# Three-product matmuls as two with [high|low] operands, and down projections in two halves of their outputs

## The chip, the cores and the metric

The kernel runs on one core of one Trainium2 chip. The metric is the device time of one execution in microseconds, the median of the runs shown. The core's engines are TensorE (PE in the profile; its weight loads have a row of their own, PEld), VectorE (DVE), ScalarE (ACT), GpSimd (POOL) and SyncE (SP), whose queue issues the weight transfers.

## The reference, cut to what matters

One sequence of 256 tokens with 1024 features passes through two layers of a first block and two layers of a second block, all in float32:

```python
# first block, per layer
x = x + concat(diff_attention, moba_attention) @ w_out
x = x + conv_ffn(rms_norm(x), w_up, conv_w, conv_b, w_down)   # silu(conv g) * (conv up), then down
# second block, per layer
x = x + 0.5 * swiglu(rms_norm_2(x), w_gate, w_up, w_down)
h = rms_norm_2(x); proj = h @ w_in + b_in
y_attn = forgetting_attention(q, k, v, log_f) @ w_o_attn
y_rnn = (rg_lru(conv(xr)) * gelu(gr)) @ w_o_rnn
x = x + (sigmoid(g_attn) * y_attn + sigmoid(g_rnn) * y_rnn) @ w_out
x = x + 0.5 * swiglu(rms_norm_2(x), ...)
```

All feed-forward layers are 2816 wide (22 tiles of 128), so there are six of them: two with the convolution and four gated ones (swiglu).

## The kernel before, in words

Activations lie with features on the partitions, in tiles of 128 features by 256 tokens. Every float32 operand of a large product is split into two float32r parts, high (a rounded copy) and low (the rest), and a product of two such operands is three matmuls that add into the same PSUM columns: high with high, high with low, low with high. `mm3` (line 419) issues them; each has its own weight load.

Weights come as a stream of chunks of 128 x 2048 float32 (1 MB), in the order in which they are used. `issue_dma` (line 234) transfers a chunk into one of NRAW = 4 raw buffers on SP's queue; `piece_h` and `piece_l` (lines 254, 268) split it in four pieces of 512 columns, the high part on ACT (tile `wh`), the low part on DVE (tile `wl`), into rings of three chunks. A raw buffer is free when its last piece is split.

- `proj` (line 529) multiplies one chunk, 8 contraction tiles by 2 output tiles, into one PSUM bank (tile `mm`): 16 calls of `mm3`. It serves the up projections (a chunk holds a gate tile and an up tile) and, in the second block's mixer, the projections x, a, n, r from the normalised operands `hH`, `hL` and the two output projections A (from `oH`) and R (from `rH`).
- `vpair` and `vproj` (lines 564, 545) multiply with the weights as the moving operand of 512, 256 or 264 columns (tile `mv`).
- `down` (line 585) adds two contraction tiles to all eight output tiles, which fill four banks (tile `acc`): again 16 calls of `mm3`. A feed-forward layer (`ffn`, line 633) alternates: two chunks up, one chunk down, the down being `lag` pairs behind (2 with the convolution, else 1). In the last chunk the order is by pairs of output tiles, and after each pair `boundary` (line 612) adds the sum to x (DVE, tile `x`), and `norm_pair` (line 480) makes the next stage's operands x*g in two parts (`xh` on ACT, `xl` on DVE) and the squares (`sq`, on ACT; their sum `ss` on POOL). The norm's factor `rstd` is applied later, when a projection's bank is read.

There are eight PSUM banks in all. During a feed-forward layer four are the accumulators and the others turn over among the up projections. After an up projection `evac_swiglu` (line 672) reads the bank once (DVE, `u<-mm,rstd`, which frees it), takes silu on ACT, multiplies on DVE and splits the result into `aH`, `aL` (`finish_act`, line 664). `make_evac_conv` (line 686) has a convolution of five more operations in between.

The order of all engines' work is written out by the program, from estimated times (class Estimate, line 69): PE's matmuls come in a fixed order, and between two tiles `substep` (line 346) puts splits and background units into the queues of ACT and DVE when the estimate says their operands are there. Each engine then runs its queue in order.

Of the kernel before, what the change touches and what calls it, by code (L numbers as in the profile page):

```python
# [25 lines left out]
NBLK = 40  # L26

# column layout of the packed per-partition vectors
# [38 lines left out]
class Estimate:  # L67
    """rough time at which each engine ends its emitted work and each tile is written:
    background work is put into the instruction streams about when its operands are there"""
# [7 lines left out]
    def key(self, x):  # L77
        """a tile, or a quarter of a chunk of weights"""
        w = self.wide.get(x.name)
        return x.name if w is None else (x.name, 4 * x.offset // w)  # L80

    def cost(self, eng, op, out, ins, kw):
# [3 lines left out]
        if eng == "pe":  # L86
            if op == "transpose":
                return 115.0
            f = 1.66 if ins[0].dtype == F32 else 0.418
            return max(107.0, f * w) + 2.0  # L90
# [53 lines left out]
def kernel(ctx: ExitStack, tc: tile.TileContext, t: dict):  # L144
# [29 lines left out]
    # ------------------------------------------------------------------ stream  # L174
    # every matrix is cut into chunks of 2048 columns per partition; a chunk is
    # loaded, split into two float32r parts, and used by the tensor engine.
    stream = []

    def phase_chunks():
        for l in range(L):  # L180
# [7 lines left out]
            ffn_chunks(t["w_up"], t["w_down"], l, 2)  # L188
        for l in range(L):
            ffn_chunks(t["w_gu1"], t["w_d1"], l, 1)  # L190
            wi = t["w_in2"]
            base = {"q": 0, "k": 4, "v": 8, "x": 12, "r": 16, "a": 20, "n": 24}
            for step in MIX2.split():
                if step == "q0":
                    stream.append(t["w_qf"][l])
                elif step == "G":
                    stream.append(t["w_g"][l])
                elif step in PAIRS:
                    stream.extend(t["w_p2"][l, PAIRS.index(step), i] for i in range(2))
                elif step[0] in "ARO":  # L200
                    stream.append(t[{"A": "w_oa", "R": "w_or", "O": "w_out2"}[step[0]]][l, int(step[1])])
                else:
                    stream.append(wi[l, base[step[0]] + int(step[1])])
            ffn_chunks(t["w_gu2"], t["w_d2"], l, 1)

    def ffn_chunks(u, d, l, lag):
        for j in range(NF // 2):
            stream.append(u[l, 2 * j])
            stream.append(u[l, 2 * j + 1])
            if j >= lag:  # L210
                stream.append(d[l, j - lag])
        for j in range(NF // 2 - lag, NF // 2):
            stream.append(d[l, j])
# [10 lines left out]
    NRAW = 4  # L224
# [6 lines left out]
    def wide(c):  # L231
        return stream[c].shape[-1]

    def issue_dma(parts=1, also=None):
# [7 lines left out]
        for i in range(parts):  # L242
            if also:
                also(i)
            nc.sync.dma_start(r[:, i * w:(i + 1) * w], stream[c][:, i * w:(i + 1) * w])
# [32 lines left out]
    def fill():  # L278
        """splits of coming chunks, as far as the vector and scalar engines have time for them"""
# [11 lines left out]
    def urgent():  # L291
        """one piece of the chunk that comes next"""
# [19 lines left out]
    # ------------------------------------------------------------- background  # L312
# [63 lines left out]
    # ----------------------------------------------------------------- consts  # L376
# [4 lines left out]
    X = [cpool.tile([P, 2, S], F32, name=f"x{i}") for i in range(4)]  # L381
    nv = VEC["early"]
# [8 lines left out]
    for p in range(4):  # L391
        est.R[X[p].name] = T0 - 500.0 + 2200.0 * p
# [16 lines left out]

    def small(w, name="sm"):  # L410
# [13 lines left out]
    # ------------------------------------------------------------------ norms  # L424
# [3 lines left out]
    def rsqrt(r, b, w):  # L428
        """r = 1 / sqrt(b + eps), with one Newton step"""
# [14 lines left out]
    def norm_tail(N):  # L444
        while N.ss is None or N.ss[1] < 4:
            yield POLL
        ssum = N.ss[0]
        (dve if N is norms[0] else pool).tensor_add(ssum[:, :S], ssum[:, :S], ssum[:, S:])
# [4 lines left out]
        pe.matmul(b[:, :S], ones_d, ssum[:, :S], start=True, stop=True)  # L453
# [4 lines left out]
        if N.tok:  # L458
            # the same by token: [token, half] and its square
# [11 lines left out]
            # eps / rstd^2: a norm of the unnormalised queries takes it in place of eps  # L471
# [8 lines left out]
    def norm_pair(N, p):  # L480
        """float32r parts of x*g of one pair of tiles, and the sum of squares"""
        yield W("act", X[p])
        xh = blk("xh", F32R)
        for m in range(2):
            act.activation(as2(xh)[:, m], X[p][:, m], AF.Identity, scale=v1(N.g, 2 * p + m))
        sq = squares(p)
        yield W("dve", xh)
        xl = blk("xl", F32R)
        for m in range(2):
            dve.scalar_tensor_tensor(as2(xl)[:, m], X[p][:, m], v1(N.g, 2 * p + m),  # L490
                                     as2(xh)[:, m].bitcast(F32), op0=ALU.mult, op1=ALU.subtract)
        N.H[p], N.L[p] = xh, xl
        add_squares(N, sq)

    def squares(p):
        sq = blk("sq")
        act.activation(sq, X[p].rearrange("p a b -> p (a b)"), AF.Square)
        return sq

    def add_squares(N, sq):  # L500
        if N.ss is None:
            N.ss = (sq, 1)
        else:
            s2 = blk("ss")
            pool.tensor_add(s2, N.ss[0], sq)
            N.ss = (s2, N.ss[1] + 1)

    def new_norm(g, tok=False):
        N = Norm()
        N.tok, N.rt, N.e2 = tok, None, None  # L510
        N.g, N.H, N.L, N.ss, N.rstd = g, [None] * 4, [None] * 4, None, None
        return N

    def k_tiles(H, Lo):
        def high(k):
            wait_for(lambda: Lo[k // 2] is not None)
            return as2(H[k // 2])[:, k % 2]
        return high, (lambda k: as2(Lo[k // 2])[:, k % 2])

    def x_update(p, acc, scale):  # L520
        xf = X[p].rearrange("p a b -> p (a b)")
        if scale == 1.0:
            dve.tensor_add(xf, acc, xf)
        else:
            dve.scalar_tensor_tensor(xf, acc, scale, xf, op0=ALU.mult, op1=ALU.add)
        unbank()

    # ------------------------------------------------------- projection kinds
    def proj(rh, rl):
        h, lo = next_chunk(None)  # L530
        h3 = h.rearrange("p (k c) -> p k c", k=KT)
        l3 = lo.rearrange("p (k c) -> p k c", k=KT)
# [3 lines left out]
        for k in range(KT):  # L536
            for m in range(2):
                ms = slice(m * P, (m + 1) * P)
                mm3(o[:, m], h3[:, k, ms], l3[:, k, ms], rh(k), rl(k),
# [5 lines left out]
    def vproj(hh, hl):  # L545
        """by token: one bank [token, half, 256], or one bank for each half of a wider chunk"""
        h, lo = next_chunk(None)
        h3 = h.rearrange("p (k c) -> p k c", k=KT)
        l3 = lo.rearrange("p (k c) -> p k c", k=KT)
# [5 lines left out]
        for k in range(KT):  # L555
            for m in range(2):
                ms = slice(m * P, (m + 1) * P)
                mm3(o[m], hh(k)[:, ms], hl(k)[:, ms], h3[:, k], l3[:, k],
# [5 lines left out]
    def vpair(hh, hl):  # L564
        """by token, 512 columns in two chunks: a bank for each half of the tokens"""
        wait_for(lambda: bank_any(2))
        bs = [bank("mv") for _ in range(2)]
        for half in range(2):
            h, lo = next_chunk(None)
            h3 = h.rearrange("p (k c) -> p k c", k=KT // 2)  # L570
            l3 = lo.rearrange("p (k c) -> p k c", k=KT // 2)
            for kk in range(KT // 2):
                k = half * (KT // 2) + kk
                for tt in range(2):
                    xh, xl = hh(k)[:, tt * P:(tt + 1) * P], hl(k)[:, tt * P:(tt + 1) * P]
# [9 lines left out]
    def down(acc, sh, sl, first, last, after=None):  # L585
        """adds two contraction tiles to all eight output tiles (four banks)"""
        h, lo = next_chunk(None)
        h3 = h.rearrange("p (k c) -> p k c", k=2)
        l3 = lo.rearrange("p (k c) -> p k c", k=2)

        def one(k, m):
            ms = slice(m * P, (m + 1) * P)
            mm3(as2(acc[m // 2])[:, m % 2], h3[:, k, ms], l3[:, k, ms], sh(k), sl(k),
# [8 lines left out]
        else:  # L602
            for p in range(4):
# [5 lines left out]
                after(p)  # L609
                substep()  # L610

    def boundary(acc, scale, N):
        """hooks for the last contraction: x update, and the next norm's operands"""
        def pair(p):
            yield W("dve", acc[p])
            if N is None:
                for m in range(2):
                    dve.scalar_tensor_tensor(X[p][:, m], as2(acc[p])[:, m], scale, X[p][:, m],
                                             op0=ALU.mult, op1=ALU.add)
                    nc.sync.dma_start(t["out"][p, :, m], X[p][:, m])  # L620
                unbank()
            else:
                x_update(p, acc[p], scale)
                yield from norm_pair(N, p)
                if p == 3:
                    spawn(norm_tail(N), front=True)

        def after(p):
            spawn(pair(p), front=True)
        return after  # L630

    # --------------------------------------------------------------------- ffn
    def ffn(N, evac, scale, N2, lag):
        rh, rl = k_tiles(N.H, N.L)
        acts = {}
        acc = []
# [985 lines left out]
```

## Time and profile before

| | us |
|---|---|
| median of 3 runs | 1920.77 |
| lowest, highest | 1915.81, 1922.2 |
| span of the profiled execution (first to last instruction; the page gives no other time of it) | 1916.7 |

In the profile, busy times of PE are of pipelined matmuls whose recorded durations overlap, so what a matmul costs is read from start to start. A timeline row gives start and duration in us, engine, line, operation, and output and inputs by the program's names; "[1.83 <-DVE xl L111]" is idle time before it and what ended it. Nearly all instructions have line 111, a recording helper, so they are told apart by their tiles.

### The profile page before, as it was taken

What the parts mean: (1) busy time and instruction counts of PE and PEld (TensorE: products, weight loads), DVE (VectorE), ACT (ScalarE), POOL (GpSimd) and SP (SyncE); (2) the same over time, 40 slices, a digit from 0 to 9 for tenths busy, and PEclk for the clock granted to TensorE, in tenths of its full rate; (3) what the DMA queues carried; (4) which work ended last, traced back from release to release, by engine and by line L of the source; (5) the groups of instructions that cost most, each with busy time, mean ns of one, the idle gap of its engine ahead of it and who ended that gap; (6) DMA issues with size and microseconds to landing.
All of it is one profiled execution on the core that took longest, in us unless ns stands there. A gap on an engine that the chain in (4) does not pass through costs nothing. (4 is left out here: it accounts for less than half of the span.)

```text
span 1916.7 us, 36939 instructions
## 1 busy us (share of the span) xinstructions
PE 1894.5 (99%) x14806; PEld 1837.7 (96%) x14806; DVE 1401.1 (73%) x2885; ACT 1170.5 (61%) x2811; POOL 58.8 (3%) x64
## 2 busy tenths in 40 slices
PE   9999999999999999999999999999999999999999
PEld 7899999899999999988999999999999899999999
DVE  7888778879878755589867755566657886866554
ACT  8866556867555644467786644454445677855443
POOL 2010001001000100010000100010001000000000
PEclk9999999999999999999999999999999999999999
DMA  9444555344555555554455455545555445545551
GB/s 290 170 154 167 186 190 184 132 155 137 196 196 176 177 176 181 193 199 165 155 186 191 173 180 184 188 156 196 177 181 208 174 154 174 181 175 198 183 191 67
DMA packets 49581, 340.05 MB, mean 177 GB/s; under 512 B 5836, under 2 KB 6900, under 8 KB 9216
## 3 DMA queue, kind: packets, MB, share of 16 engines
q1 hardware_dynamic: 47808, 330.19, 49.8%
q0 software_dynamic: 1456, 7.47, 1.4%
q8 instruction: 116, 1.90, 0.4%
q14 instruction: 57, 0.47, 0.1%
q10 hardware_dynamic: 144, 0.02, 0.0%
HBM read 336.30 MB, written 1.36 MB: 176 GB/s over the span
## 5 line engine op out<-in xcount | busy, mean ns | idle before, releaser
L111 ACT ACTIVATE wh<-raw 128x512 fp32r<-128x512 f32 x1248 | 709.4, 627 | 546.3 <-PE mm L111 203.9
L111 DVE TENSOR_TENSOR wl<-raw,wh 128x512 fp32r<-128x512 f32 x1248 | 807.3, 691 | 195.5 <-ACT wh L111 194.4
L111 PE MATMUL mm<-xl,wh 128*128 128x256 f32 x2112 | 600.4, 284 | 10.8 <-DVE xl L111 10.8
L111 PE MATMUL mm<-xh,wh 128*128 128x256 f32 x2112 | 601.5, 285 | 0.0
L111 PE MATMUL mm<-xh,wl 128*128 128x256 f32 x2112 | 599.9, 284 | 0.0
L111 PEld LDWEIGHTS mm<-xl,wh 128*128 128x128 f32 x2112 | 407.6, 193 | 12.4 <-DVE xl L111 12.0
L111 PEld LDWEIGHTS mm<-xh,wh 128*128 128x128 f32 x2112 | 407.7, 193 | 0.4
L111 PEld LDWEIGHTS mm<-xh,wl 128*128 128x128 f32 x2112 | 407.6, 193 | 0.0
L111 PE MATMUL acc<-aH,wh 128*128 128x256 f32 x1056 | 298.8, 283 | 0.0
L111 PE MATMUL acc<-aL,wh 128*128 128x256 f32 x1056 | 298.8, 283 | 0.0
L111 PE MATMUL acc<-aH,wl 128*128 128x256 f32 x1056 | 298.8, 283 | 0.0
L111 DVE TENSOR_TENSOR u<-mm,rstd 128x512 f32<-128x512 f32 x132 | 90.8, 691 | 223.6 <-PE mm L111 223.6
L111 PEld LDWEIGHTS acc<-aH,wh 128*128 128x128 f32 x1056 | 202.8, 192 | 0.0
L111 PEld LDWEIGHTS acc<-aL,wh 128*128 128x128 f32 x1056 | 202.8, 192 | 0.0
L111 PEld LDWEIGHTS acc<-aH,wl 128*128 128x128 f32 x1056 | 202.8, 192 | 0.0
L111 PE MATMUL mv<-wh,xl 128*128 128x512 f32 (+2 forms) x416 | 157.8, 379 | 3.3 <-DVE xl L111 3.3
L111 PE MATMUL mv<-wh,xh 128*128 128x512 f32 (+2 forms) x416 | 160.4, 386 | 0.2 <-ACT wh L111 0.2
L111 PE MATMUL mv<-wl,xh 128*128 128x512 f32 (+2 forms) x416 | 155.9, 375 | 0.0
L111 PE MATMUL mm<-hH,wh 128*128 128x256 f32 x512 | 145.9, 285 | 0.0
L111 PE MATMUL mm<-hH,wl 128*128 128x256 f32 x512 | 144.9, 283 | 0.0
L111 PE MATMUL mm<-hL,wh 128*128 128x256 f32 x512 | 144.8, 283 | 0.0
L111 PEld LDWEIGHTS mm<-hL,wh 128*128 128x128 f32 x512 | 98.2, 192 | 0.1
(218 smaller groups left out, 2789.5 us busy)
## 6 DMA issues: line engine op xcount, KB each, us to landing
raw<-in_w_gu SPq DMA_DIRECT2D x88, 1024.0 KB, 4.9
raw<-in_w_up SPq DMA_DIRECT2D x44, 1024.0 KB, 4.8
raw<-in_w_d SPq DMA_DIRECT2D x44, 1024.0 KB, 4.8
raw<-in_w_p SPq DMA_DIRECT2D x42, 1024.0 KB, 5.1
raw<-in_w_in SPq DMA_DIRECT2D x34, 1024.0 KB, 4.9
raw<-in_w_down SPq DMA_DIRECT2D x22, 1024.0 KB, 4.9
raw<-in_w_out SPq DMA_DIRECT2D x16, 1024.0 KB, 4.9
raw<-in_w_oa SPq DMA_DIRECT2D x8, 1024.0 KB, 4.9
```

Source lines behind the costliest of these rows:

```text
L111: f(*a, **k)
```

## The change

- `mm2` takes the place of `mm3` in most projections: the moving operand holds [high|low] side by side, 512 columns, so one matmul with the high weights makes high-high and high-low in two halves of a bank, and a second one of 256 columns adds low-high to the second half. The two halves are added when the bank is read. `proj2` uses it for the swiglu layers' up projections and the mixer's x, a, n, r, A and R; it needs two banks per chunk where `proj` needs one. The convolution's up projections keep `proj`, the first mixer's output projection keeps `down`, and the value and query projections are as before.
- An output tile of a down projection now needs a bank of its own, eight for all; so `down2` computes four output tiles at a time. All six feed-forward layers and the second mixer's last projection run it in two passes: the first half of the outputs in between the up projections (now in groups of four contraction tiles), the second half after them, from activations that are all kept. The chunks of these weights are half rows of two old chunks, read in runs of 512 columns by two transfers; the last group has half a chunk.
- Reading a bank: `add_parts` (ACT copies one half, DVE adds the other, for both output tiles) or `add_bias` comes first, and frees the banks without waiting for `rstd`. x is updated per tile, from two halves.
- Operands of the next stage are made per tile, and squares are added per tile on POOL, at the start of the kernel too, where DVE added them before.
- NRAW is 3, the pool of blocks has 41 buffers for 40, and six half blocks are new. The last projection O comes after all of R. The estimate's matmul times are changed.

```diff
-    NRAW = 4
+    NRAW = 3
...
-            "A0 A1 A2 A3 R0 R1 O0 R2 O1 R3 O2 O3")
+            "A0 A1 A2 A3 R0 R1 R2 R3 O0 O1 O2 O3")
...
+    def half_rows(w, half, g):
+        v = w[2 * g:min(2 * g + 2, w.shape[0])].rearrange("c p (k m) -> p c k m", k=2)
+        return v[:, :, :, half * 512:(half + 1) * 512]
+
+    def ffn_order(lag):
+        left = list(range(NG))
+        for j in range(NF):
+            yield "up", j
+            while left and 4 * left[0] + 3 + lag <= j:
+                yield "dn", (0, left.pop(0))
+        for g in left:
+            yield "dn", (0, g)
+        for g in [NG - 1, *range(NG - 1)]:
+            yield "dn", (1, g)
...
     def add_squares(N, sq):
         if N.ss is None:
             N.ss = (sq, 1)
         else:
-            s2 = blk("ss")
-            pool.tensor_add(s2, N.ss[0], sq)
+            pool.tensor_add(N.ss[0], N.ss[0], sq)
...
+    def mm2(b, lh, ll, x, start, stop):
+        pe.matmul(b, lh, x, start=start, stop=False, skip_group_check=True)
+        pe.matmul(lo(b), ll, hi(x), start=False, stop=stop, skip_group_check=True)
...
+    def add_parts(t, bs):
+        yield W("act", *bs)
+        for m in range(2):
+            act.activation(as2(t)[:, m], lo(bs[m]), AF.Copy)
+        yield W("dve", t)
+        for m in range(2):
+            dve.tensor_add(as2(t)[:, m], hi(bs[m]), as2(t)[:, m])
+            unbank()
...
+    def down2(acc, R, ks, half_, first, last, after):
+        h, l_ = next_chunk(None)
+        h3 = h.rearrange("p (k c) -> p k c", c=512)
+        l3 = l_.rearrange("p (k c) -> p k c", c=512)
+        def one(i, m):
+            ms = slice(m * P, (m + 1) * P)
+            mm2(acc[m], h3[:, i, ms], l3[:, i, ms], R.both(ks[i]), first and i == 0, last and i == len(ks) - 1)
+        if not last:
+            for i in range(len(ks)):
+                for m in range(4):
+                    one(i, m)
+                    substep()
+        else:
+            for m in range(4):
+                for i in range(len(ks)):
+                    one(i, m)
+                    if i < len(ks) - 1:
+                        substep()
+                after(4 * half_ + m, [hi(acc[m]), lo(acc[m])])
+                substep()
...
-    def evac_swiglu(N, b, j, a):
+    def evac_swiglu(N, bs, j, tiles):
+        u = blk("u")
+        yield from add_parts(u, bs)
         while N.rstd is None:
             yield POLL
-        yield W("dve", b, N.rstd)
-        u = blk("u")
-        dve.tensor_mul(as2(u), as2(b), rep2(N.rstd))
-        unbank()
+        yield W("dve", u, N.rstd)
+        dve.tensor_mul(as2(u), as2(u), rep2(N.rstd))
...
-            ffn(norms[2 * l + 1], make_evac_conv(l), 1.0, norms[2 * l + 2], 2)
+            ffn(norms[2 * l + 1], make_evac_conv(l), 1.0, norms[2 * l + 2], 4, proj)
...
-            ffn(norms[o], evac_swiglu, 0.5, norms[o + 1], 1)
+            ffn(norms[o], evac_swiglu, 0.5, norms[o + 1], 2, proj2)
```

## Rows read from the trace of the kernel before

**Rows 1.** The page's head: span, then busy time, share and instructions of each engine.

```profile
span 1916.7 us, 36939 instructions
PE 1894.5 (99%) x14806; PEld 1837.7 (96%) x14806; DVE 1401.1 (73%) x2885; ACT 1170.5 (61%) x2811; POOL 58.8 (3%) x64
```

**Rows 2.** Waits: engine and tile, releaser, us in total, times, longest.

```profile
PE mm L111 <- DVE xl L111: 10.8, 6, 1.8
PEld mv L111 <- DVE xl L111: 3.7, 2, 1.9
```

**Rows 3.** Timeline of PE in steady 256-column work, first and last of 33 matmuls.

```profile
1000.04 0.28 PE L111 MATMUL mm<-hL,wh 128*128 128x256 f32 x1
...
1003.88 0.28 PE L111 MATMUL mm<-hH,wh 128*128 128x256 f32 x1
```

**Rows 4.** Timeline of PE in steady 512-column work, first and last of 28 matmuls.

```profile
11.73 0.39 PE L111 MATMUL mv<-wl,xh 128*128 128x512 f32 x1
...
17.85 0.39 PE L111 MATMUL mv<-wl,xh 128*128 128x512 f32 x1
```

**Rows 5.** Timeline of PE where 512 columns are followed by 256.

```profile
902.30 0.39 PE L111 MATMUL mv<-wl,xh 128*128 128x512 f32 x1
902.52 0.28 PE L111 MATMUL mm<-hH,wh 128*128 128x256 f32 x1
902.64 0.28 PE L111 MATMUL mm<-hL,wh 128*128 128x256 f32 x1
```

**Rows 6.** Matmul groups by form, the first product of each three: count, busy us, mean ns, idle.

```profile
L111 PE MATMUL mm<-xh,wh 128*128 128x256 f32 x2112 | 601.5, 285 | 0.0
L111 PE MATMUL acc<-aH,wh 128*128 128x256 f32 x1056 | 298.8, 283 | 0.0
L111 PE MATMUL mm<-hH,wh 128*128 128x256 f32 x512 | 145.9, 285 | 0.0
L111 PE MATMUL mm<-oH,wh 128*128 128x256 f32 x128 | 36.2, 283 | 0.0
L111 PE MATMUL mm<-rH,wh 128*128 128x256 f32 x128 | 36.2, 283 | 0.0
L111 PE MATMUL acc<-mH,wh 128*128 128x256 f32 x128 | 36.2, 283 | 0.0
```

**Rows 7.** DMA issues of the gated layers' up weights: count, size, us to landing.

```profile
raw<-in_w_gu SPq DMA_DIRECT2D x88, 1024.0 KB, 4.9
```

**Rows 8.** Windows: PE, PEld, DVE, ACT, POOL busy (x), PEclk, DMA, GB/s; boundary, then swiglu.

```profile
1084.70:1088.10 3.40, 3.40 (x17) 3.31 (x16) 2.48 (x5) 1.23 (x3) 0.00 (x0) 0.50 0.60 195
...
650.00:812.00 162.00, 162.00 (x1352) 162.00 (x1352) 95.45 (x174) 75.97 (x152) 0.00 (x0) 1.00 0.54 183
```

**Rows 9.** Tile x in one swiglu layer, 634 to 828 us: ns min/median/max.

```profile
L111 DVE SCALAR_TENSOR_TENSOR xl<-x,vec,xh x8: 471/475/1542, 635.5 to 826.9; 128x256 fp32r<-128x256 f32 x8
L111 ACT ACTIVATE xh<-x,vec x8: 491/494/510, 821.2 to 826.6; 128x256 fp32r<-128x256 f32 x8
```

**Rows 10.** Timeline: two halves of a bank read by ACT, two by DVE.

```profile
1003.36 0.84 ACT L111 ACTIVATE sg<-mm,vec 128x256 f32<-128x256 f32 x2 [1.12 <-PE mm L111]
...
1908.61 0.76 DVE L111 SCALAR_TENSOR_TENSOR x<-acc,x 128x256 f32<-128x256 f32 x2 [4.69 <-PE acc L111]
```

**Rows 11.** Timeline of DVE after a convolution layer's last up projection.

```profile
302.27 0.69 DVE L111 TENSOR_TENSOR u<-mm,rstd 128x512 f32<-128x512 f32 x1 [0.84 <-PE mm L111]
...
311.32 0.42 DVE L111 TENSOR_TENSOR aL<-s,aH 128x256 fp32r<-128x256 f32 x1
```

**Rows 12.** Timeline of DVE after a swiglu layer's last up projection.

```profile
812.87 0.69 DVE L111 TENSOR_TENSOR u<-mm,rstd 128x512 f32<-128x512 f32 x1 [1.99 <-PE mm L111]
...
816.30 0.42 DVE L111 TENSOR_TENSOR aL<-s,aH 128x256 fp32r<-128x256 f32 x1
```

**Rows 13.** The kernel's start, DVE's last sum of squares; then POOL's sums by form.

```profile
18.31 0.42 DVE L111 TENSOR_TENSOR sq<-sq 128x256 f32<-128x256 f32 x1
...
L111 POOL TENSOR_TENSOR ss<-ss 128x256 f32<-128x256 f32 x9 | 9.3, 1039 | 0.7
```

More of the change, by code (lines that the diff above doesn't have):

```diff
@@ L408, in blk, with half @@
         return blkp["p"].tile(list(shape), dt, tag="blk", name=nm(name))
+    def half(name):
+        return blkp["p"].tile([P, S], F32, tag="half", bufs=6, name=nm(name))
     def small(w, name="sm"):
@@ L452, in norm_tail @@
         b = bank("st")
-        pe.matmul(b[:, :S], ones_d, ssum[:, :S], start=True, stop=True)
+        pe.matmul(b[:, :S], ones_d, ssum, start=True, stop=True)
         yield W("act", b)
@@ L478, in norm_tail, with xt, hi, lo @@
             N.e2 = rt[:, 2:4]
[L480 to L492, printed above, removed]
+    def xt(k):
+        return X[k // 2][:, k % 2]
+    def hi(a):
+        return a[:, :S]
+    def lo(a):
+        return a[:, S:]
+    def norm_tile(N, k):
+        yield W("act", xt(k))
+        a = blk("xs", F32R)
+        act.activation(hi(a), xt(k), AF.Identity, scale=v1(N.g, k))
+        sq = squares(k)
+        yield W("dve", a)
+        dve.scalar_tensor_tensor(lo(a), xt(k), v1(N.g, k), hi(a).bitcast(F32), op0=ALU.mult, op1=ALU.subtract)
+        N.X[k] = a
         add_squares(N, sq)
-    def squares(p):
-        sq = blk("sq")
-        act.activation(sq, X[p].rearrange("p a b -> p (a b)"), AF.Square)
+    def squares(k):
+        sq = half("sq")
+        act.activation(sq, xt(k), AF.Square)
         return sq
@@ L510, in new_norm, with __init__, both, high @@
         N.tok, N.rt, N.e2 = tok, None, None
-        N.g, N.H, N.L, N.ss, N.rstd = g, [None] * 4, [None] * 4, None, None
+        N.g, N.X, N.ss, N.rstd = g, [None] * KT, None, None
         return N
[L514 to L525, printed above, removed]
-        unbank()
-    def proj(rh, rl):
-        h, lo = next_chunk(None)
+    class Ops:
+        def __init__(self, tiles):
+            self.tiles = tiles
+        def both(self, k):
+            wait_for(lambda: self.tiles[k] is not None)
+            return self.tiles[k]
+        def high(self, k):
+            return hi(self.both(k))
+        def low(self, k):
+            return lo(self.both(k))
+    def proj(R):
+        h, l_ = next_chunk(None)
         h3 = h.rearrange("p (k c) -> p k c", k=KT)
-        l3 = lo.rearrange("p (k c) -> p k c", k=KT)
+        l3 = l_.rearrange("p (k c) -> p k c", k=KT)
         wait_for(bank_any)
@@ L583, in vpair, with down @@
         return bs
-    def down(acc, sh, sl, first, last, after=None):
-        h, lo = next_chunk(None)
+    def down(acc, R, first, last, after=None):
+        h, l_ = next_chunk(None)
         h3 = h.rearrange("p (k c) -> p k c", k=2)
-        l3 = lo.rearrange("p (k c) -> p k c", k=2)
+        l3 = l_.rearrange("p (k c) -> p k c", k=2)
         def one(k, m):
             ms = slice(m * P, (m + 1) * P)
-            mm3(as2(acc[m // 2])[:, m % 2], h3[:, k, ms], l3[:, k, ms], sh(k), sl(k),
+            mm3(as2(acc[m // 2])[:, m % 2], h3[:, k, ms], l3[:, k, ms], R.high(k), R.low(k),
                 first and k == 0 and m % 2 == 0, last and k == 1 and m % 2 == 1)
@@ L608, in down @@
                             substep()
-                after(p)
+                after(2 * p, [as2(acc[p])[:, 0]], False)
+                after(2 * p + 1, [as2(acc[p])[:, 1]])
                 substep()
-    def boundary(acc, scale, N):
-        def pair(p):
-            yield W("dve", acc[p])
-            if N is None:
[L617 to L621, printed above, removed]
-            else:
-                x_update(p, acc[p], scale)
-                yield from norm_pair(N, p)
-                if p == 3:
+    def down2(acc, R, ks, half_, first, last, after):
+        h, l_ = next_chunk(None)
+        h3 = h.rearrange("p (k c) -> p k c", c=512)
+        l3 = l_.rearrange("p (k c) -> p k c", c=512)
+        def one(i, m):
+            ms = slice(m * P, (m + 1) * P)
+            mm2(acc[m], h3[:, i, ms], l3[:, i, ms], R.both(ks[i]), first and i == 0, last and i == len(ks) - 1)
[4 more added lines that the diff above has]
+                    substep()
+        else:
+            for m in range(4):
[4 more added lines that the diff above has]
+                after(4 * half_ + m, [hi(acc[m]), lo(acc[m])])
+                substep()
@@ new lines, in boundary, with tile_ @@
+    def boundary(scale, N):
+        def tile_(k, parts, free):
+            for a in parts:
+                yield W("dve", a)
+                if scale == 1.0:
+                    dve.tensor_add(xt(k), a, xt(k))
+                else:
+                    dve.scalar_tensor_tensor(xt(k), a, scale, xt(k), op0=ALU.mult, op1=ALU.add)
+            if free:
+                unbank()
+            if N is None:
+                nc.sync.dma_start(t["out"][k // 2, :, k % 2], xt(k))
+            else:
+                yield from norm_tile(N, k)
+                if k == KT - 1:
@@ L664, in finish_act, with after, ffn @@
-    def finish_act(av, j, a):
-        yield W("act", av)
-        act.activation(as2(a.H)[:, j % 2], av, AF.Copy)
-        yield W("dve", a.H)
-        dve.tensor_sub(as2(a.L)[:, j % 2], av, as2(a.H)[:, j % 2].bitcast(F32))
-        a.n += 1
-    def evac_swiglu(N, b, j, a):
+        def after(k, parts, free=True):
+            spawn(tile_(k, parts, free), front=True)
+        return after
+    def ffn(N, evac, scale, N2, lag, mul):
+        R = Ops(N.X)
+        A = Ops([None] * NF)
+        acc = [[], []]
+        for what, j in ffn_order(lag):
+            if what == "up":
+                spawn(evac(N, mul(R), j, A.tiles))
+                substep()
+            else:
+                half_, g = j
+                ks = range(4 * g, min(4 * g + 4, NF))
+                wait_for(lambda: all(A.tiles[k] is not None for k in ks))
+                first = not acc[half_]
+                if first:
+                    wait_for(lambda: bank_any(4))
+                    acc[half_] = [bank("acc") for _ in range(4)]
+                down2(acc[half_], A, ks, half_, first, g == NG - 1 - half_, boundary(scale, N2))
@@ L1118, in mix1 @@
                 n_o += 1
-                down(acc, lambda k: o.H[:, k], lambda k: o.L[:, k], n_o == 1, n_o == 4, boundary(acc, 1.0, N2))
+                down(acc, Ops(o.tiles), n_o == 1, n_o == 4, boundary(1.0, N2))
     def ln1p_small(e, q, p):
@@ L1281, in sig_unit @@
     def sig_unit(b, cols, box, ready):
-        yield W("act", b)
         box.s = blk("sg")
-        if not ready():
-            for m in range(2):
-                act.activation(as2(box.s)[:, m], as2(b)[:, m], AF.Identity, bias=cols[m])
-            unbank()
-            while not ready():
-                yield POLL
-            fn(box.s, box.s, AF.Sigmoid)
-        else:
-            for m in range(2):
-                fn(as2(box.s)[:, m], as2(b)[:, m], AF.Sigmoid, bias=cols[m])
-            unbank()
+        yield from add_bias(box.s, b, cols)
+        while not ready():
+            yield POLL
+        yield W("act", box.s)
+        fn(box.s, box.s, AF.Sigmoid)
         box.ready = True
```

302 lines of the change are left out of this document (145 added, 157 removed).

## The prediction, made blind

> **What bounds the kernel now.** I read the page's head first: TensorE is busy 99% of the span, DVE 73%, ACT 61% [rows 1]. A busy PE only says that matmuls overlap, so the second reading is who waits for whom. PE waits almost only for the low part of the next stage's operands (tile xl), at stage boundaries: six waits of up to 1.8 us under `mm`, two under `mv`, some 14.5 us in all (10.8 us, and 3.7 us on the weight load's row) [rows 2]. Third, the timeline: in steady work matmuls start at an even step and nothing stands between them. 33 matmuls of 256 columns take 3.84 us from first to last start, 120.0 ns each [rows 3]; 28 of 512 columns take 6.12 us, 226.7 ns each [rows 4]. The 256 further columns cost 106.7 ns, 2.4 columns per ns, so both sizes carry the same fixed 13.3 ns (120.0 - 106.7; 226.7 - 213.3). In a stretch of a swiglu layer 1352 records fill 162 us: 119.8 ns each at full clock, with DVE busy for 95 us and ACT for 76 us [rows 8]. The bound is PE's issue of matmuls, plus eight boundaries.
>
> **Term 1, the matmuls.** A tile costs 3 x 120.0 = 360.0 ns now. After the change it is one matmul of 512 and one of 256 columns: 226.7 + 120.0 = 346.7 ns, 13.3 ns less, the fixed part of the matmul that goes. The columns are the same 768. Converted tiles: 88 gated up chunks [rows 7] x 16 = 1408 of the 2112 in `mm<-xh` (the convolution's 704 stay), the six down projections 1056, hH 512, oH 128, rH 128, mH 128 [rows 6]: 3360. 3360 x 13.3 ns = **44.8 us**, all on the path. No row has 512 and 256 columns in alternation. The nearest is a change from one to the other, with starts 0.22 and then 0.12 us apart [rows 5]: 0.34 us for the pair, to 10 ns a row. So the pair lies between 0.34 us (saves 20 ns, 67 us in all) and the three matmuls' 0.36 us (saves nothing; a switch cost that eats the whole fixed part). I take 346.7, which both steady steps give.
>
> The rows put a fixed 13.3 ns on each matmul. The Trainium skill, "TensorE: Matmul & The Clock Gate", section "Back-to-back issue gap", has the step as columns / 2.4 plus about 2.5 ns at full clock; by that the change would save only 3360 x 2.5 = 8.4 us, an estimate from that page. The trace disagrees with it at both sizes (120.0 and 226.7 ns), and the measurement decides.
>
> **Term 2, the boundaries.** Six of the eight waits follow a down projection that is now done in halves (four swiglu layers less the last, two mixers, the second convolution). There the first four operand tiles are ready a whole pass early, and the last four become due one by one, a tile each 4 x 346.7 = 1.39 us. After the last matmul, tile 7 needs two updates of x (0.76 us for two such reads [rows 10]), its high part (0.49 us on ACT) and its low part on DVE, 0.48 us as a median but up to 1.54 [rows 9]: 1.7 to 2.8 us, or 4.0 with two weight splits of 0.6 ahead of it. The next stage asks for it after 7 x 2 x 346.7 ns = 4.9 us. So the wait can go: 4 x 1.8 + 2 x 1.85 = 10.9 us. With it goes the half clock: after such a wait PE made 17 matmuls in 3.4 us [rows 8], 1.4 us lost; I count three such windows behind these six waits, 4.2 us. Upper end 15 us, lower end 0; I take **12 us**, leaving a rest for splits queued ahead. The two boundaries after the first mixer keep `down` and stay: 0.
>
> **Term 3, new waits.** (a) The convolution layers' last up tile: DVE starts on its bank at 302.27 and ends the low part at 311.74, 9.5 us later, weight splits included [rows 11]. Before, two more chunks (11.5 us) cover that. Now 16 + 4 tiles lie between, 20 x 346.7 = 6.9 us: PE waits 2.5 us, twice, **+5 us** (0 to 9: nothing if splits give way, 4.5 each with a half-clock window behind it). (b) The swiglu layers' last tile took 3.9 us [rows 12]; two ACT copies (0.84) and two DVE adds (0.76) [rows 10] make it 5.5 us under the same 6.9: 0 (to +1 each). The mixer's last product, before O's second group, is of the same kind: 0 (to +1 each). (c) At the start the sum of squares ends on DVE at 18.7 us [rows 13]. Now seven sums run on POOL, 1.04 us each, nearest row of that width [rows 13]: 7.3 us from about 15.6, so 4.2 us later, while the estimate that places the product has POOL faster. **+2 us** (0 to 4), PE waiting in order.
>
> **What costs nothing, and its cover.** Reading a converted chunk adds 0.84 us on ACT and 0.76 on DVE [rows 10], for 88 + 32 + 16 = 136 chunks 114 and 103 us; with x in halves DVE comes to about 1530 us and ACT to 1290, under 1870. In the swiglu stretch DVE goes from 95 to about 110 of 157 us. PE would see it only where a bank or a split comes late. Four banks are left beside the accumulators, two projections' worth; the third projection needs the first one's banks 16 x 346.7 = 5.5 us after its end, and the read takes 1.6 us plus queueing. I add **+1 us** for this and all else (0 to 5). Three raw buffers: a chunk lands 4.9 us after its issue [rows 7] and is split two chunks later, some 11 us; even a doubled time for half rows in two transfers on SP's queue would fit. If that cover went, each miss would show as ACT waiting for `raw`. 41 blocks hold 22 activations, 8 operands and the tiles in work.
>
> **The sum.** -44.8 - 12 + 5 + 2 + 1 = -48.8 us. The profiled span 1916.7 becomes 1867.9. The median of the runs lies 4.1 us above that span and I carry this over: **1872 us**.
>
> **Rivals.** *Waits stay.* Term 1 comes, but splits ahead of xl keep the boundary waits and the tails take their upper ends: 1920.8 - 44.8 + 9 + 4 + 3 = 1892 us (1884 to 1900). For it: xl's spread to 1.54 us, and POOL now sums twice as often; against it: the first half's tiles are early whatever happens. *A cheaper pair.* 0.34 us: 22 us more, 1850; only 10 ns rows speak for it. *The change doesn't do what it says.* The alternation eats the fixed part, 0.36 us per tile: term 1 is nothing and terms 2 and 3 are as forecast, 1920.8 - 12 + 8 = 1917 us; against it, the rows at the change of sizes show no such cost [rows 5]. The 2.5 ns of the Trainium skill's "TensorE: Matmul & The Clock Gate" would end near this rival, at an estimated 1908 us. *Slower: banks.* In the swiglu layers the projection waits for the two banks of the one before the last, since ACT and DVE queue the copy and the add behind splits. Some 68 up chunks start with the accumulators held; to be slower by 5.8 us they would have to wait 54.6 / 68 = 0.8 us each, that is, the read would have to end 6.3 us after the chunk. At 1 us each it is 1940 us. For it: two engines in a row where one was enough. Against it: DVE now starts on such a bank 0.03 us after PE's last product [rows 12], and it idles 40% of this stage [rows 8].
>
> **How the numbers follow.** Chances: forecast 0.64 (its own range 1860 to 1884), waits stay 0.19, cheaper pair 0.08, no saving 0.04, banks 0.05. Runs of this kernel can tell a difference of about 0.3%, 5.8 us. The first three are faster: 0.91; the fourth is the same: 0.04; the last slower: 0.05. The range 1856 to 1895 takes in the forecast and most of the waits case, and leaves out the other three, 0.17, and a little of the tails.
>
> **What would show it.** Right: 11446 matmuls; starts in a swiglu layer alternating so that a pair takes 346 to 348 ns; PE's waits for the operands' low part gone but for the two boundaries after the first mixer; one wait of some 2.5 us at the end of each convolution layer's up projections, for that layer's last activations; a wait of 1 to 3 us near 19 us for the sum of squares. Wrong: a pair of 355 ns or more; PE waiting for a bank at the start of up chunks, released by DVE's add; DVE at 90% in the swiglu layers; boundaries that still show 1.8 us and a half clock.

## The result, and the profile after

| | before | after |
|---|---|---|
| median of 4 runs each, us | 1918.72 | 1894.95 |
| lowest, highest | 1915.81, 1922.2 | 1892.23, 1898.76 |
| span of the profiled execution | 1916.7 | 1891.8 |

The ratio is 0.988, 95% interval 0.986 to 0.9901: 23.8 us less. The forecast was 48.8 us less; the time lies at the very end of the stated range (1856 to 1895). The matmuls gave most of what they were said to give, and the boundaries more than that, so new losses took about half of it back.

The head of the page of the changed kernel, and two of its groups (busy us, mean ns, then idle time just before them):

```profile
span 1891.8 us, 31179 instructions
PE 1857.2 (98%) x11446; PEld 1652.2 (87%) x11446; DVE 1523.7 (81%) x3301; ACT 1258.8 (67%) x3123; POOL 69.0 (4%) x98
...
L112 PE MATMUL mm<-xs,wh 128*128 128x256 f32 (+1 forms) x2816 | 745.5, 339 | 2.8 <-DVE xs L112 2.8
...
L112 PE MATMUL mm<-hS,wh 128*128 128x512 f32 x512 | 185.8, 406 | 16.7 <-DVE ge L112 16.7
```

3360 matmuls are gone [rows 1]. The waits for the low part of the operands, 10.8 us [rows 2], are down to 2.8 us under `mm<-xs`. But `mm<-hS`, the projections of the second block's mixers, which had waited 0.0 us [rows 6], now waits 16.7 us.

Timeline of PE in a gated layer of the changed kernel, first and last of 11 pairs:

```profile
699.84 0.39 PE L112 MATMUL acc<-as,wh 128*128 128x512 f32 x1
700.07 0.28 PE L112 MATMUL acc<-as,wl 128*128 128x256 f32 x1
...
703.66 0.39 PE L112 MATMUL mm<-xs,wh 128*128 128x512 f32 x1
```

11 pairs take 3.82 us, 347 ns each: forecast 346.7. This holds in all four gated layers, but not everywhere. In the down projection of a convolution layer of the same kernel, the first and last of 11 starts:

```profile
599.86 0.40 PE L112 MATMUL acc<-as,wh 128*128 128x512 f32 x1
...
603.39 0.40 PE L112 MATMUL acc<-as,wh 128*128 128x512 f32 x1
```

10 pairs take 3.53 us, 353 ns each. So do the second block's projections A, R and O; x, a, n and r take 350 ns on average. Three matmuls of 256 columns take 360 ns in all these places (experiment four). Why some stretches are slower is open.

PE's waits in the changed kernel, all of over 0.6 us (us in total, times, longest):

```profile
PE mm L112 <- DVE ge L112: 16.7, 2, 8.4
PE qt L112 <- DVE qn L112: 7.2, 1, 7.2
PE mm L112 <- DVE xs L112: 2.8, 4, 0.9
PE warm L994 <- DVE vp L112: 2.0, 1, 2.0
PE st L112 <- POOL sq L112: 1.3, 1, 1.3
```

The first two are new. To see their whole price, I took every start of a matmul in both traces: what the step to the next start exceeds columns / 2.4 + 13.3 ns by counts as lost (idle time, half clock and slower pairs together). The lost time rises from 54.0 to 74.0 us, while the columns and fixed parts, which follow from the counts by this rule, fall from 1856.7 to 1812.0. A boundary is counted as the first 11 us of the stage behind it:

| us | forecast | found |
|---|---|---|
| matmuls by their count (term 1) | -44.8 | -44.7 |
| pairs slower than 346.6 ns (term 1) | 0 | +6.9 |
| six boundaries (term 2) | -12 | 17.6 to 1.3, -16.3 |
| convolution tails (term 3a) | +5 | 0 |
| start and first mixer of layer 1, with the boundary behind it (term 3c) | +2 | 14.2 to 24.0, +9.8 |
| second block's two mixers, without the rows above (in "all else", +1) | +1 | 11.0 to 33.0, +22.0 |
| rest | 0 | 11.2 to 8.9, -2.3 |
| sum | -48.8 | -24.6 (spans: -24.9) |

**The mixers.** Timeline of PE, ACT and DVE of the changed kernel around the first 8.4 us:

```profile
988.08 0.28 PE L112 MATMUL mm<-hS,wl 128*128 128x256 f32 x1
996.72 0.77 PE L112 MATMUL mm<-hS,wh 128*128 128x512 f32 x1 [8.37 <-DVE ge L112]
...
1002.62 0.54 PE L112 MATMUL mm<-hS,wh 128*128 128x512 f32 x1
```

```profile
990.53 0.71 ACT L112 ACTIVATE th<-th,tiny 128x512 f32<-128x512 f32 x1
991.27 0.63 ACT L112 ACTIVATE th<-th 128x512 f32<-128x512 f32 x1
991.80 3.01 ACT L112 ACTIVATE ge<-mm,vec 128x256 f32<-128x256 f32 x8
...
994.39 1.27 DVE L112 TENSOR_TENSOR_SCAN z<-r,yc 128x256 f32<-128x256 f32 x2
995.58 0.67 DVE L112 SCALAR_TENSOR_TENSOR th<-z,th 128x512 f32<-128x512 f32 x1
996.16 2.07 DVE L112 TENSOR_TENSOR ge<-mm,ge 128x256 f32<-128x256 f32 x6
```

The four r projections (tile `ge`) take two banks each, all eight. Their copies stand behind the recurrence (`th`, `z`) in ACT's queue and start at 991.80, all eight at once; DVE's adds start at 996.16, 0.56 us before PE goes on. In the kernel before, r took one bank a chunk and was read later still, but the other four banks carried the projections that followed (timeline of ACT of the kernel before):

```profile
1013.59 1.57 ACT L111 ACTIVATE ge<-mm,vec 128x256 f32<-128x256 f32 x4
```

Windows of the changed kernel, the wait and what follows (busy us and instructions of PE, PEld, DVE, ACT, POOL, then PEclk, DMA share, GB/s):

```profile
988.20:996.60 8.40, 0.16 (x2) 0.00 (x0) 8.33 (x15) 7.42 (x17) 0.00 (x0) 0.77 0.63 235
996.70:1002.70 6.00, 5.98 (x19) 5.13 (x20) 5.96 (x14) 5.23 (x9) 0.00 (x0) 0.50 0.00 1
```

After the idle time PE runs at a granted clock of 0.50, the 1.2 GHz level: 9 pairs from 996.72 to 1002.62 take 5.90 us for 9 x 347 ns = 3.12. This place so costs 8.4 + 2.8 = 11.2 us. The second, from 1614.8 us on, costs 8.4 us of waiting and 2.0 at half clock; the two are nearly all of the 22.0 us.

**The start.** PE and ACT of the changed kernel, then windows of it and of the kernel before:

```profile
49.65 2.35 PE L112 MATMUL qt<-cst,qn 128*128 128x128 f32 x8 [7.21 <-DVE qn L112]
...
41.15 1.15 ACT L112 ACTIVATE wh<-raw 128x512 fp32r<-128x512 f32 x2 [2.76 <-DMA raw<-in_w_p]
...
46.86 2.19 ACT L112 ACTIVATE wh<-raw 128x512 fp32r<-128x512 f32 x4 [2.89 <-DMA raw<-in_w_p]
```

```profile
21.00:28.00 7.00, 6.27 (x28) 5.24 (x29) 5.43 (x15) 7.00 (x42) 1.69 (x3) 1.00 0.82 172
28.00:42.00 14.00, 14.00 (x64) 11.57 (x63) 6.85 (x18) 8.12 (x42) 3.91 (x8) 1.00 1.00 221
```

```profile
21.00:28.00 7.00, 6.75 (x29) 4.97 (x28) 3.68 (x9) 6.99 (x41) 0.00 (x0) 1.00 0.99 405
28.00:42.00 14.00, 14.00 (x65) 11.56 (x64) 13.30 (x38) 12.43 (x56) 4.34 (x8) 1.00 0.95 193
```

From 26 to 29 us on, the attention's bias tables are gathered on POOL's queue. In all seven traces read there (both kernels and experiments three, five, six, eight and nine) only 191 to 221 GB/s move from 28 to 42 us, with the DMA engines busy. What differs is what has moved before: 405 GB/s x 7 us = 2.8 MB before, 172 x 7 = 1.2 MB after. The chunks that are still to come meet the gather, ACT waits for `raw`, and the query's norm (`qn`) stands behind those splits. The Trainium skill, "DMA: Bandwidth & Descriptors", section "Issuing engines are not separate DMA queues", says that transfers share the same 16 engines whichever engine starts them. The windows agree: with the gather and the weights together the engines are 95 and 100% busy in the two kernels.

### The profile page after: what moved, and what is told of

Same layout as the page of the kernel before. It is cut to its first block, busy times and chain, and to the rows that moved or that the text cites. A ratio compares the mean times of both kernels' runs of the same rounds, so it can differ in the third digit from the quotient of the medians.

```text
span 1891.8 us, 31179 instructions
## 1 busy us (share of the span) xinstructions
PE 1857.2 (98%) x11446; PEld 1652.2 (87%) x11446; DVE 1523.7 (81%) x3301; ACT 1258.8 (67%) x3123; POOL 69.0 (4%) x98
## 4 chain that ended last, share of the span: by engine, by line
PE 92%; ACT 3%; DVE 3%; DMA 2%; issue 0%; SPq 0%; ACTq 0%
PE mm L112 51%; PE acc L112 23%; PE mv L112 13%; DMA raw<-in_w_p 2%; PE av L112 1%; DVE wl L112 1%; PE s L112 1%; ACT wh L112 1%; PE qt L112 1%; PE pt L112 1%; ACT r L112 1%; ACT th L112 1%; DVE xs L112 0%; DVE z L112 0%; DVE yc L112 0%
## 5 line engine op out<-in xcount | busy, mean ns | idle before, releaser
L112 PE MATMUL mm<-xs,wh 128*128 128x256 f32 (+1 forms) x2816 | 745.5, 339 | 2.8 <-DVE xs L112 2.8
L112 PE MATMUL mm<-xs,wl 128*128 128x256 f32 x2112 | 591.4, 280 | 0.0
L112 PEld LDWEIGHTS mm<-xs,wh 128*128 128x128 f32 x2816 | 483.6, 189 | 64.4 <-DVE xs L112 3.6
L112 PEld LDWEIGHTS mm<-xs,wl 128*128 128x128 f32 x2112 | 399.7, 189 | 0.1
L112 PE MATMUL acc<-as,wh 128*128 128x512 f32 x1056 | 369.8, 395 | 0.0
L112 PE MATMUL acc<-as,wl 128*128 128x256 f32 x1056 | 294.9, 279 | 0.0
L112 PE MATMUL mv<-wh,xs 128*128 128x512 f32 (+2 forms) x832 | 255.2, 384 | 0.0
L112 PEld LDWEIGHTS acc<-as,wh 128*128 128x128 f32 x1056 | 198.4, 188 | 46.1
L112 PE MATMUL mm<-hS,wh 128*128 128x512 f32 x512 | 185.8, 406 | 16.7 <-DVE ge L112 16.7
L112 PEld LDWEIGHTS acc<-as,wl 128*128 128x128 f32 x1056 | 199.3, 189 | 0.0
L112 PEld LDWEIGHTS mv<-wl,xs 128*128 128x128 f32 x416 | 78.5, 189 | 13.3 <-DVE wl L112 0.3
```

Of the source, the lines that this page charges most:

```text
L112: f(*a, **k)
```

## The experiments

**One: the reads of r ahead.** Are the mixer's waits a matter of when the banks are read?

```diff
-            spawn(gelu_unit(proj2(H_), j, l, R))
+            spawn(gelu_unit(proj2(H_), j, l, R), front=True)
```

> The changed kernel with the units that read the four r projections put ahead of the other background work, as boundary units are; nothing else. Theory 'banks': in the second block's mixer the four r projections fill all eight PSUM banks, because their reads stand in ACT's and DVE's queues behind the recurrence, so the next projection waits 8.4 us in each of the two layers and some 10 us at half clock follow. With the reads ahead both waits and both half-clock stretches go: about 12 us a layer, 24 in all, span near 1868 us, and the only wait of PE over 1.5 us is the one near 42 us. Theory 'too much work': ACT and DVE simply have more to do there than PE leaves time for; then the recurrence comes later by what was put ahead of it, and PE waits as long at A or R, or in n2 and n3: span 1885 to 1895 us.

1888.56 us, ratio 0.9836 (0.9819 to 0.9853). PE's waits in the mixers:

```profile
PE mm L112 <- ACT wh L112: 4.6, 2, 2.3
PE acc L112 <- DVE sp L112: 3.7, 3, 1.8
```

The wait for `ge` is gone, and smaller ones come later, for weight splits and for the last product's operands: the work moved ahead pushed those back. The order is not the cure. By its expectation this run speaks for 'too much work' (span 1888.4 us); the next one decides between the two theories.

**Two: r in one bank.** r goes back to `proj` and to the unit of the kernel before, 128 matmuls more (+1.7 us).

```diff
-            spawn(gelu_unit(proj2(H_), j, l, R))
+            spawn(gelu_unit(proj(H_), j, l, R))
...
-        yield from add_bias(ge, b, [v1(("bin", l), 32 + 2 * j + m) for m in range(2)])
         while R.nh < 4:
             yield POLL
-        yield W("act", ge, R.h[j])
-        fn(ge, ge, AF.Gelu_apprx_tanh)
+        yield W("act", b, R.h[j])
+        for m in range(2):
+            fn(as2(ge)[:, m], as2(b)[:, m], AF.Gelu_apprx_tanh, bias=v1(("bin", l), 32 + 2 * j + m))
+        unbank()
```

> The changed kernel with the four r projections alone as before: three matmuls into one bank each, and gelu reading the bank when the recurrence is done. Theory 'banks': four banks are taken and four stay for n2 and n3, so the waits go although the banks are held for longer: span near 1870 us (24 us less for the waits, 2 x 4 x 16 x 13.3 ns = 1.7 us more for the matmuls). Theory 'too much work': the copies and adds of all other projections are still there, only those of r are gone, so at least half of the waits stays: span 1880 us or more.

1874.23 us, 0.977 (0.9752 to 0.9787). Waits of PE, all above 0.6 us:

```profile
PE qt L112 <- DVE qn L112: 5.1, 1, 5.1
PE mm L112 <- DVE xs L112: 2.8, 4, 0.9
PE warm L994 <- DVE vp L112: 2.0, 1, 2.0
PE st L112 <- POOL sq L112: 1.3, 1, 1.3
```

No wait for `ge`; the two mixers lose 12.2 us, where they lost 11.0 before and 33.0 after. The time falls by 20.7 us, although 128 matmuls more are made: the banks were the miss in the mixers.

**Three: three raw buffers alone, in the kernel before.**

```diff
-    NRAW = 4
+    NRAW = 3
```

> The kernel before with three raw buffers for four; nothing else. Theory 'buffers': the 7.2 us wait near 42 us in the changed kernel comes from weights that are asked for one chunk later and so run into the transfers of the bias tables; then the kernel before gets a wait of 4 to 10 us of the same kind before 60 us (ACT waiting for raw weights by some 3 us more than now), and with a half clock behind it the span grows by 4 to 12 us, to 1921 to 1929; after 60 us nothing changes by over 2 us. Theory 'sums on POOL': the wait comes from the sum of squares, which is unchanged here: span within 2 us of 1916.7.

1930.05 us, 1.0053 (1.0038 to 1.0068) of its before's 1920.39. A window of it, and what the splits of `raw` waited for in the first 64 us (DVE for ACT, ACT for the DMA; us, times):

```profile
21.00:28.00 7.00, 6.74 (x29) 4.94 (x28) 3.66 (x9) 6.99 (x41) 1.57 (x3) 1.00 0.86 227
```

```profile
  ACT wh L111: 17.4, 6
  DMA raw<-in_w_p: 14.9, 6
```

ACT's waits for `raw` go from 3.5 to 14.9 us, PE waits 8.1 us for `qn`, and the lost time of the start and the first mixer goes from 14.2 to 28.2 us, while all other stages together lose 1.5 us less. So the number of buffers by itself can make the start's miss; on the median it is 9.7 us.

**Four: the changed kernel with three products.** Term 1 undone alone.

```diff
-        pe.matmul(b, lh, x, start=start, stop=False, skip_group_check=True)
+        pe.matmul(hi(b), lh, hi(x), start=start, stop=False, skip_group_check=True)
+        pe.matmul(lo(b), lh, lo(x), start=False, stop=False, skip_group_check=True)
         pe.matmul(lo(b), ll, hi(x), start=False, stop=stop, skip_group_check=True)
```

> The changed kernel with each pair of matmuls issued as three of 256 columns into the same columns; nothing else. Theory 'fixed part': each matmul carries 13.3 ns beside its columns, in alternation too: 3360 more matmuls are 44.8 us; the mixer's waits get shorter by some 1 to 2 us as PE is slower: span 1933 to 1938 us. Theory 'alternation': the change of sizes costs some of it already, and three equal ones give it back: span below 1920 us. Steps of 120 ns in place of 232 and 117.

1932.8 us, 1.0071 (1.0056 to 1.0086): span 40.7 us over that of the changed kernel: columns and fixed parts are 44.7 us more, the lost time 4.0 less, since the slower pairs are gone with the alternation. The six boundaries lose 1.5 us in all, where they lost 17.6 before, so the halves of the outputs took the boundary waits away, not the cheaper pairs. The mixers' two waits stay and grow from 16.7 to 18.2 us, against the expectation.

**Five: four raw buffers in the changed kernel.** The room comes from the blocks.

```diff
-NBLK = 41
+NBLK = 38
-    NRAW = 3
+    NRAW = 4
-        return blkp["p"].tile([P, S], F32, tag="half", bufs=6, name=nm(name))
+        return blkp["p"].tile([P, S], F32, tag="half", bufs=4, name=nm(name))
```

> The changed kernel with four raw buffers for three; to make room, 38 blocks for 41 and four half blocks for six. Theory 'buffers': the wait of 7.2 us near 42 us and the 6.8 us of half clock behind it go, 8 to 10 us in all; the mixers' two waits of 8.4 us stay: span 1881 to 1885 us. Theory 'sums on POOL': the start stays as it is, since the sum of squares still ends 3 us later than in the kernel before: span 1889 to 1894. If the lack of three blocks costs something, it shows as new waits elsewhere.

1891.62 us, 0.9852 (0.9838 to 0.9867): no gain that counts. The wait for `qn` is 3.2 us, but others come beside it, and the start loses 24.6 us. A miss for theory 'buffers'; the span, 1891.7 us, is that of 'sums on POOL'.

**Six: one bank and four raw buffers**, the edits of two and five together.

> Both repairs together: r projections in one bank each with three matmuls, and four raw buffers (38 blocks, four half blocks). If the two causes are apart, their gains add: 1874.2 less 8 to 10 us, a time of 1864 to 1867 us, and no wait of PE over 2 us is left but those at the boundaries behind the first mixer. If one of them only moved the other, the time stays over 1870 us.

1871.01 us, 0.9751 (0.9735 to 0.9767), within the spread of the second. Its ACT at the start shows a reason why the buffer alone does not help:

```profile
16.57 0.42 ACT L112 ACTIVATE sq<-x 128x256 f32<-128x256 f32 x1 [0.24 <-POOL sq L112]
17.40 0.42 ACT L112 ACTIVATE sq<-x 128x256 f32<-128x256 f32 x1 [0.41 <-POOL sq L112]
18.22 0.42 ACT L112 ACTIVATE sq<-x 128x256 f32<-128x256 f32 x1 [0.40 <-POOL sq L112]
```

With four half blocks the squares wait for POOL's sums of 0.8 us, and ACT, in order, keeps the weight splits behind them back. These waits are some 1.5 us in all; that they make the whole loss of the start is argued, not shown. From 21 to 28 us 332 GB/s move here, and ACT still waits 4.4 us for `raw`.

**Seven: the convolution's up projections with two matmuls too** (on top of the second). The one place that the change leaves alone.

```diff
-            ffn(norms[2 * l + 1], make_evac_conv(l), 1.0, norms[2 * l + 2], 4, proj)
+            ffn(norms[2 * l + 1], make_evac_conv(l), 1.0, norms[2 * l + 2], 4, proj2)
...
-        def evac(N, b, j, tiles):
+        def evac(N, bs, j, tiles):
+            u = blk("u")
+            yield from add_parts(u, bs)
             while N.rstd is None:
                 yield POLL
-            yield W("dve", b, N.rstd)
-            u = blk("u")
-            dve.tensor_mul(as2(u), as2(b), rep2(N.rstd))
-            unbank()
+            yield W("dve", u, N.rstd)
+            dve.tensor_mul(as2(u), as2(u), rep2(N.rstd))
```

> The kernel with r in one bank each (e2_r_one_bank), and the convolution's up projections made of two matmuls as well, with the copy and the add ahead of the rest. Theory 'matmuls decide everywhere': 704 tiles x 13.3 ns = 9.4 us less, a time near 1865 us. Theory 'DVE decides there': in the convolution's up stretch DVE is busy 109 of 122 us in the changed kernel; 18 more chunks' adds of 0.7 us bring it to 122 while PE's share falls to 118, so the gain is lost or more: 1873 to 1885 us, with PE waiting for banks or for the layer's activations, released by DVE.

1890.16 us, 0.9841 (0.9825 to 0.9857), 16 us over the second. Waits of PE, and the window of a convolution layer:

```profile
PE mm L112 <- ACT as L112: 8.4, 2, 4.2
...
PE acc L112 <- DVE as L112: 6.3, 2, 3.3
```

```profile
146.00:268.00 122.00, 117.80 (x671) 103.10 (x670) 113.69 (x237) 87.02 (x191) 0.00 (x0) 0.99 0.53 181
```

PE waits for the activations under `acc`. Under `mm` it waits for a bank: the profile names ACT's `as`, which an up projection does not read, but the wait ends as DVE's first add, which frees the bank, is done:

```profile
211.54 1.41 DVE L112 TENSOR_TENSOR u<-mm,u 128x256 f32<-128x256 f32 x4
...
212.10 0.47 PE L112 MATMUL mm<-xs,wh 128*128 128x512 f32 x1 [4.20 <-ACT as L112]
```

DVE is busy 113.7 of 122 us: here the reading of two halves is on the path, and 704 tiles x 13.3 ns = 9.4 us of matmuls don't pay for it.

**Eight: the start's squares summed on DVE again** (on top of the second).

```diff
-            add_squares(N0, squares(k))
+            sq = squares(k)
+            if k:
+                dve.tensor_add(N0.ss[0], N0.ss[0], sq)
+            N0.ss = (N0.ss[0] if k else sq, k + 1)
```

> The one-bank kernel, with the start's eight squares summed on DVE again as in the kernel before. Theory 'sums': POOL's seven additions at the start delay POOL's queue and with it the gather of the bias tables, so that weight chunks 6 and 7 meet it later and longer; with the sums on DVE the loss of the first 64 us goes from 23 back toward the 14 us of the kernel before, and the time from 1874 to about 1866 us. Rival 'buffers alone': three raw buffers hold the start's chunks back whoever sums; the wait for qn of 7 us stays and the time is 1872 to 1877 us.

1875.87 us, 0.9782 (0.9767 to 0.9796). The product of the sums starts at 19.13 for 21.69 us, but PE waits 9.0 us for `qn` and ACT 13.7 us for `raw`: nothing won with three buffers, as the rival said.

**Nine: the same with four raw buffers**, the edits of five and eight and one bank for r.

> The same with four raw buffers (38 blocks, four half blocks). Theory 'both': the start needs the fourth buffer and the sums on DVE together; the first 64 us lose 14 to 16 us as in the kernel before, no wait for qn over 2 us, and the time is about 1864 us. Rival 'neither': what delays the start is the order of the work itself (splits and operands per tile), the loss stays at 22 to 25 us and the time is 1870 to 1874 us.

1863.76 us, 0.9718 (0.9702 to 0.9735) of 1917.38. Windows of its start, and ACT's waits there:

```profile
21.00:28.00 7.00, 7.00 (x32) 5.79 (x31) 4.27 (x10) 6.99 (x42) 0.28 (x1) 1.00 0.99 378
28.00:42.00 14.00, 14.00 (x64) 11.54 (x63) 13.15 (x38) 12.42 (x56) 4.05 (x8) 1.00 0.99 210
```

```profile
ACT wh L112 <- DMA raw<-in_w_p: 0.9, 3, 0.4
```

The wait for `qn` is gone and the start loses 12.7 us (before: 14.2). Each of the two edits alone brings 3 us or nothing, both bring 10.5: with three buffers the chunks come late, with POOL's sums the fourth buffer is filled but not emptied in time (the second half of this is argued from the rows of experiment six). The profiles of experiments six, eight and nine have one gated layer each whose pairs take 353 ns, 3.3 us that the second run's profile lacks, so differences of 3 us between these runs need not be the start's. Whether POOL's sums would do with four raw buffers and all six half blocks was not tried. This is the fastest version of the study, 53.6 us under the kernel before, 31 under the changed one.

## Why the prediction was right and where it failed

- **Term 1, right in its step, and 6.9 us too large**: 346.7 ns a pair in the gated layers, as forecast, but 350 to 353 in the convolutions' down projections and in the second block's mixers. On average a pair takes 348.7 ns, so the term gave some 38 us for 44.8. Experiment four, 40.7 us slower, gives about the same from the other side. The Trainium skill, "TensorE: Matmul & The Clock Gate", section "Back-to-back issue gap", gives columns / 2.4 + 2.5 ns for an isolated matmul, and for a stream of weight loads and matmuls some 131 ns at 512 columns. The trace agrees with neither (226.7 ns); its 13.3 ns hold.
- **Term 2, right, and larger**: of the boundary waits only those after the first block's two mixers are left, four of at most 0.9 us under `mm`, as said. The six others gave 16.3 us for 12, a little over the upper end of 15.
- **Term 3a, mis-sized**: +5 us for the convolutions' tails, found 0. Between the bank and the low part [rows 11] stood eight weight splits of 0.6 us, and I kept them. Now four of half the columns, 0.42 us each, are in between: DVE starts on the last bank at 288.59 and ends at 294.02 us, 5.4 us, under the 6.9 of the matmuls. The lower end, "nothing if splits give way", is what came:

```profile
288.59 0.69 DVE L112 TENSOR_TENSOR u<-mm,rstd 128x512 f32<-128x512 f32 x1 [1.37 <-PE mm L112]
...
293.60 0.42 DVE L112 TENSOR_TENSOR as<-y,as 128x256 fp32r<-128x256 f32 x1 [0.48 <-ACT as L112]
```

- **Term 3c, right in itself, and not what the start lost**: PE waits 1.3 us for the sum. In DVE's place POOL did more harm once a fourth buffer was there, some 7 us between experiments six and nine, which differ in the sums alone; that it came through ACT's queue is argued.
- **"What costs nothing", the raw buffers: failed.** The cover was "a chunk lands 4.9 us after its issue", the median of the gated layers [rows 7]. In the changed kernel's first 64 us it was (the view of tile `raw`, transfers of 0.25 and 1 MB together):

```profile
DMA to landing us min/median/max: 3.2/7.1/17.0
```

  The long ones fall together with the bias tables' gather. The step was read from a stage with free DMA engines and used for one without. The kernel before shows 3.5/8.5/16.6 in the same 64 us, so the trace at hand already had it. The sign named for it, ACT waiting for `raw`, is what the trace shows; its price is some 10 us (experiments three and nine).
- **"What costs nothing", the banks: failed, and it is the larger part.** The count of two projections' worth of banks beside the accumulators is that of a feed-forward layer, and there it holds: DVE is busy 109.7 of 145 us in a gated layer and PE waits for no bank. The mixer was not looked at. There the read is not 1.6 us "plus queueing" after its chunk; the four r chunks follow each other and end at 988.2 us, so the first ended 3 x 16 x 347 ns = 16.7 us earlier, at 971.5; its copy starts at 991.80, 20 us later, since ACT runs the recurrence first. The rival with the banks had the right wait, DVE's add, in the wrong place, and priced it by 68 small waits where two large ones came: 22.0 us in the mixers, with the half clock behind the waits, where "all else" had 1.

With both covers put back (experiment nine) the span is 55.1 us under that of before, 6 more than the forecast. That does not prove the sum: the tails did not come (5 us), the boundaries and the start gave some 8 us more than forecast, and the slower pairs and r's third matmuls took some 9 us back.

That the time lies within the range is luck. It also lies in the range of the rival "waits stay" (1884 to 1900), but the boundary waits that this rival kept are gone; what cost the time stood under "What costs nothing".

## What to carry to other kernels

When a change doubles the banks that a result holds, go through every stage in which such results wait for something other than their reader being free, and count the banks there; results that wait long should keep the narrow form. A buffer that is taken away has to be checked against the slowest landing of its stream, not the median, and the two cures of one stall can each look useless until both are in.

## What the runs showed of the hardware that was not expected

- In the alternation the fixed part is not shared evenly: the start after a 512-column matmul comes a median 232 ns later, after a 256-column one 117 ns later, where steady work has 226.7 and 120.0.
- The step of a pair is the same over a whole stretch, but not everywhere: 346.7 ns in the gated layers of the changed kernel, 353 in its convolutions' down projections and in A, R and O. In experiment nine one gated layer takes 353 and A, R and O take 346.7. No run here shows the reason.
- While the bias tables are gathered, the 16 DMA engines are busy 95% of the time and move 193 GB/s in the kernel before, where the stretch ahead had 405 GB/s at 99%; in the changed kernel they are busy 100% and move 221. A busy share of DMA says little about bytes.
- After 8.4 us without a matmul PE stayed at the 1.2 GHz level (granted clock 0.50) for 5.9 us of full work, at the second place for some 4 us; the two places cost 4.8 us beside their idle time of 16.7.
